# The sixth conditioning part moved into the output projection, the fifth spread over the last attention group, and earlier weight splits in the first stage

## The chip, the core and the metric

The kernel runs on one core of a Trainium2 chip. The metric is device time of one execution in microseconds (us), the median of several runs. Engines: TensorE does matrix products and transposes (PE in the profile, PEld its weight loads), VectorE is DVE, ScalarE is ACT, GpSimd is POOL, and SyncE (SP) issues most of the transfers from memory. Each engine works through its own instructions in the order in which they stand in its queue, and waits at an instruction whose inputs or buffers aren't ready.

## The reference, cut to what matters

One layer of a decoder for 512 prompt tokens and 8 x 4 sample tokens, 544 columns in all, with 1024 features. A conditioning vector c (one for the prompt, eight for the samples, nine in all) gives six modulation vectors:

```python
ada = jnp.einsum('bd,dn->bn', jax.nn.silu(c), lp['w_ada']) + lp['b_ada']
sh_m, sc_m, gt_m, sh_f, sc_f, gt_f = [a[:, None, :] for a in jnp.split(ada, 6, axis=-1)]
h = rms_norm(x, g[0]) * (1.0 + sc_m) + sh_m
y, st = mixer(h)                                  # projections, attention, convolution, merge, w_out
x = x + gt_m * rms_norm(y, g[1])
h = rms_norm(x, g[2]) * (1.0 + sc_f) + sh_f
a, b = jnp.split(jnp.einsum('btd,df->btf', h, lp['w_ffn_in']), 2, axis=-1)
y = jnp.einsum('btf,fd->btd', jax.nn.silu(a) * b, lp['w_ffn_out'])
x = x + gt_f * rms_norm(y, g[3])
```

`w_ada` is 1024 x 6144, 25 MB. Its six column blocks are the six conditioning parts, 0 to 5. Part 4 (sc_f, the fifth) is first needed in the second norm, after the output projection. Part 5 (gt_f, the sixth) is first needed when the last product of the feed-forward network is written out.

## The kernel before, in words

Data lie with features on the partitions and the 544 columns along the free dimension, in two halves of 272. Weights come as tiles of 128 x 1024 f32 (512 KB), through one ring, `RING`: a list of (planned time, kind, number), sorted by planned time. The tiles are loaded strictly in the ring's order. Each takes one of three `wraw` buffers (`NB = 3`); the odd conditioning tiles of parts 2 and 3 have a buffer of their own, `xraw`. The planned times are of a plan, not of the chip: TO, the start of the output projection in the plan, is 543.8, while its first products run near 579 us in the trace.

There are two sorts of ring tile:

- Weights of the big projections (glu, kv, g, pw2, q, gb, ga, out, fi, fo) are split in two before use: ACT writes a rounded high half `wh` (line 168), DVE the rest `wl` (line 171). Two `wh` and two `wl` buffers exist (the kept output tiles 5, 6 and 7 have three more of their own, which lie in memory that the attention gives back). A product of a half tile is 24 matmuls: high weights by high and low activations, then low weights by high activations. The `wraw` buffer is free for the next load when both halves are written.
- Raw tiles (`ada`, the conditioning tiles; `qs`; and a few more) are used by PE as they came. A conditioning tile is four 32-column matmuls (eight records in the trace) of the conditioning vectors by the tile. The buffer is free when PE is done with them. Eight tiles make a part: their sums collect in one buffer of PSUM that the part holds from its first to its last tile. Then ACT copies it (`adaz`, line 319), PE transposes the copy (`turn`), and DVE adds the bias into `adaT` (line 353).

What runs when is set by a heap of planned events: each step of each piece of work is a Python function with a planned time, and the instructions are emitted in the order of those times. In emission order earlier instructions have precedence; the final order on each engine can differ a little, since an instruction whose inputs are not expected yet is passed by others. The ring's bookkeeping runs along with the emission: `take` hands out the next tile, splits it if it isn't yet, and splits the next weight tile ahead if at most one raw tile lies between. `raw_done` gives a raw tile's buffer back. After a conditioning tile, `split_upto(rst["use"])` splits the next tile of the ring if that is a weight tile. `load_more` issues loads while there are buffers.

Around the change in time:

- First stage, to about 235 us: glu, kv and gate projections, a convolution of 31 steps for each of four channel groups on DVE (line 711), compression of cached pages, parts 2 and 3 and the `qs` tiles.
- Four attention groups (235 to 601 us). In each, four `unit`s of 128 rows: scores on PE into the two `big` buffers, mask and maximum on DVE (lines 1106, 1107), exponentials on ACT (line 1110), which free the `big` buffers, scaling (line 1118), transposes (line 1138, again into `big`), copies (lines 1139, 1140), products with the values into `pv`. Projections gb, ga, q and conditioning tiles are emitted between these steps. In the last group these are parts 4 and 5, with their sums in one of the two `mm` buffers.
- Output projection (from 579 us, overlapping the last unit): tiles `out0` 0 to 7 for the first column half, then the second half with kept tiles 5, 6, 7 (no loads) and `out1` 0 to 4. Their results go to `mm`. When the attention's memory is given back, SP loads x again (`load_x`, four transfers). The second norm and the feed-forward network follow.

Of the kernel before, what the change touches and what calls it, by code (L numbers as in the profile page):

```python
# [56 lines left out]
def at(g, x):  # L57

    t = TA + 14 + sum(GL[:g])
    return t + x * GL[g] / 10 if x <= 10 else t + GL[g] + (x - 10) * 6.4  # L60


TO = at(3, 10.345)
# [12 lines left out]
def fo_entry(ft, kg):  # L76
    return (ft // 4 * 3 + kg) * 4 + ft % 4


def _plan():  # L80

    p = [(1 + 0.1 * n, "glu", n) for n in range(NG)]
    p += [(2.345 + 0.089 * n, "ada", n) for n in range(8, 12)]
    p += [(45.047 + 6.5 * (n - NG), "glu", n) for n in range(NG, 8)]
    p += [(76.104 + 10.023 * n, "kv", n) for n in range(12)]
    p += [(60.955 + 4.999 * n, "ada", 16 + n) for n in range(16)]
    p += [(at(3, 1.557 + 0.388 * n), "ada", 32 + n) for n in range(16)]
    p += [(164.548, "g", 0)]
    p += [(203.02 + 3.438 * n, "pw2", n) for n in range(8)]
    p += [(114.735 + 9.994 * n, "qs", n) for n in range(8)]  # L90
    p += [(TA + 6.676 * n, "q", n) for n in range(2)]
    for g in range(4):
        if g < 3:
            p += [(at(g, 6.173 if g == 0 else 5.336), "q", 2 * g + 2), (at(g, 9.783) - 1.608, "q", 2 * g + 3)]
        p += [(at(g, 12.132 + 0.267 * n) if g < 3 else at(3, 0.308 + 0.745 * n), "ga", 2 * g + n) for n in range(2)]
    for n, (g, x) in enumerate(((0, 1.6), (0, 3.4), (0, 4.8), (0, 8.0), (1, 4.5), (1, 7.7), (2, 4.5), (2, 7.7))):
        p += [(at(g, x), "gb", n)]
    p += [(TO + 3.069 * n, "out0", n) for n in range(8)]
    p += [(TO + 31.9 + 2.718 * n, "out1", n) for n in range(5)]
    p += [(TO + 50.404 + 3 * NF * hf + 2.986 * n, "fi%d" % hf, n) for hf in range(2) for n in range(NF)]  # L100
    p += [(TS + 0.008 * n, "sf", n) for n in range(NF, 44)]
    p += [(TG + 64.062 * hf + 7.662 * ft + 3.08 * kg, "fo%d" % hf, fo_entry(ft, kg))
          for hf in range(2) for ft in range(8) for kg in range(3)]
    return [(t + 1e-4 * i, kind, n) for i, (t, kind, n) in enumerate(sorted(p))]


RING = _plan()
WHEN = {e[1:]: e[0] for e in RING}
KV_ORDER = [0, 1, 2, 4, 3, 5]
# [3 lines left out]
def body(ctx, tc, xT, cT, cst, sel, vecs, b1row, wall, w1, pool_rows, kwin, vwin, convst, ptab,  # L113
# [6 lines left out]
    def ev(t, f, *a):  # L120
        count[0] += 1
        heapq.heappush(heap, (t, count[0], f, a))
# [44 lines left out]
    def hi(dst, src, scale=1.0):  # L167
        act.activation(dst, src, AF.Copy, scale=scale)  # L168

    def lo(dst, src, h, eng=None):  # L170
        (eng or dve).tensor_sub(dst, src, h.bitcast(F32))  # L171
# [20 lines left out]
    def is_raw(j):  # L192
        _, kind, n = RING[j]
        return kind in ("ada", "qs", "sf") or kind == "glu" and n < NG

    raws, splits = {}, {}
    rst = {"load": 0, "split": 0, "use": 0}

    def entry(i):

        _, kind, n = RING[i]
        kind = kind.rstrip("01")
        if kind == "ada":
            return wall[n // 2][:, (n % 2) * 1024:(n % 2) * 1024 + 1024], 1024
        if kind == "fo":
            part, m = divmod(n, 4)
            k = FO_K[part % 3][1] * 128
            return wall[FIRST["wfo"] + part * 2 + m // 2][:, (m % 2) * k:(m % 2) * k + k], k
        k = 512 if kind == "pw2" else 1024
        kind = {"qs": "q", "sf": "fi"}.get(kind, kind)  # L210
        per = 1 if kind == "g" else 2048 // k
        return wall[FIRST["w" + kind] + n // per][:, (n % per) * k:(n % per) * k + k], k
# [4 lines left out]
    def load_more(end=len(RING)):  # L217

        while rst["load"] < end:
            j = rst["load"]  # L220
            _, kind, n = RING[j]
            own = kind == "ada" and 15 < n < 32 and n % 2
            pl, tag, bufs = (xr, "xraw", 1) if own else (wp, "wraw", NB)
            if j < 4 + NG and j % 3:
                pl, tag, bufs = late_pools["araw"], "araw", 5
            if kind == "sf" and (n - NF) % 4 == 3:
                pl, tag, bufs = late_pools["sraw"], "sraw", 1
            if out[tag] == bufs:
                break
            out[tag] += 1  # L230
            rst["load"] = j + 1
            src, k = entry(j)
            raw = pl.tile([128, 1024], F32, name=tag, tag=tag, bufs=bufs)
            if j == 6 + NG:
                load_w1()
            nc.sync.dma_start(raw[:, :k], src)
            raws[j] = raw, k, tag

    def raw_done(*tags):
        for tag in tags:  # L240
            out[tag] -= 1
        load_more()

    def split_upto(i):
        while rst["split"] <= min(i, len(RING) - 1):
            j = rst["split"]
            rst["split"] = j + 1
            if is_raw(j):
                continue
            raw, k, tag = raws.pop(j)  # L250
            out[tag] -= 1
            own = RING[j][1] == "out0" and RING[j][2] in KEPT
            h, l = ((kp if own else wp).tile([128, 1024], F32R, name=w, tag=w, bufs=3 if own else 2) for w in ("wh", "wl"))
            hi(h[:, :k], raw[:, :k])
            m = 640 if RING[j][1] in () else k
            lo(l[:, :m], raw[:, :m], h[:, :m])
            if m < k:
                lo(l[:, m:k], raw[:, m:k], h[:, m:k], pool)
            splits[j] = h.rearrange("p (k m) -> p k m", m=128), l.rearrange("p (k m) -> p k m", m=128)

    def take(kind, n):

        i = rst["use"]
        rst["use"] = i + 1
        assert RING[i][1:] == (kind, n), (RING[i], kind, n)
        if is_raw(i):
            return raws.pop(i)[::2]
        split_upto(i)
        j = i + 1
        while j < len(RING) and is_raw(j):  # L270
            j += 1
        if j - i <= NB - 1:
            split_upto(j)
        load_more()
        return splits.pop(i)

    def when(kind, n):
        return WHEN[kind, n]
# [33 lines left out]
    def ada_product(p, k, raw):  # L312

        for q in range(4):
            mm(p[32 * q:32 * q + 32, 0:256], cs[:, k], raw[:, q * 256:q * 256 + 256], k == 0, k == 7)

    def ada_quarters(p):
        z = hp.tile([128, 256], F32, name="adaz", tag="adaz", bufs=2)
        act.activation(z, p[:, 0:256], AF.Copy)
        return z  # L320
# [7 lines left out]
    def ada_bias(part):  # L328
        return vc[:, V_BADA + 8 * part:V_BADA + 8 * part + 8].rearrange("p (q a) -> p a q", a=2)
# [6 lines left out]
        dve.tensor_add(adaT[:, 0:2, 2 * qt:2 * qt + 2], t, bias.to_broadcast([128, 2, 2, 9]))  # L336
        return ins

    def ada_part(part, bank):

        def step(k):
            raw, tag = take("ada", 8 * part + k)
            if k == 0:
                ada_ps[part] = bank()
            ada_product(ada_ps[part], k, raw)
            raw_done(tag)
            split_upto(rst["use"])
            if k == 7:
                z = ada_quarters(ada_ps.pop(part))
                ev(when("ada", 8 * part + 7) + 4.968, turn, z)  # L350

        def turn(z):
            dve.tensor_add(adaT[:, part].rearrange("p (q a) b -> p a q b", a=2), ada_turned(z)[1],
                           ada_bias(part)[:, :, :, None].to_broadcast([128, 2, 4, 9]))

        for k in range(8):
            ev(when("ada", 8 * part + k), step, k)
# [3 lines left out]
    def modulation(dst, part, gi, plus1):  # L361
        gb = gains[:, gi, :, None].to_broadcast([128, 8, 9])
        if plus1:
            dve.scalar_tensor_tensor(dst, adaT[:, part], 1.0, gb, op0=OP.add, op1=OP.mult)
        else:
            dve.tensor_mul(dst, adaT[:, part], gb)
# [76 lines left out]
    def load_w1():  # L443
        for kd in range(2):
            t_ = xp.tile([128, 2048], F32, name="w1t", tag="w1t%d" % kd)
            nc.sync.dma_start(t_, w1[:, kd])
            w1t.append(t_.rearrange("p (l m) -> p l m", m=128))
# [502 lines left out]
    n = 0  # L950
# [13 lines left out]
    for part in (2, 3):  # L964
        ada_part(part, half_big)
# [339 lines left out]
                                dst = dst.rearrange("p (b t) -> p b t", t=4)  # L1305
                                act.activation(dst, v[64 * h2:64 * h2 + 64, :, pr, h2, 2 * jj + jp, :], AF.Copy)

    for part in (4, 5):
        ada_part(part, P_mm)
    for f in range(8):  # L1310
        ev(when("q", f), q_tile, f)
        gb_tile(f)
# [76 lines left out]
    A2 = yp.tile([128, 8, 9], F32, name="A2")  # L1389
    G3 = yp.tile([128, 8, 9], F32, name="G3")  # L1390
    modulation(A2, 4, 2, True)
    modulation(G3, 5, 3, False)
    uh, ul = {}, {}
    h2p = ctx.enter_context(tc.tile_pool(name="h2p", bufs=1))
    h2h = h2p.tile([128, 8, T], F32R, name="h2h", tag="h2h")
# [166 lines left out]
    raw, split, bank, keep = {}, {}, {}, {}  # L1562
# [273 lines left out]
```

## Time and profile before

| | |
|---|---|
| time, median of 3 runs | 1038.76 us (1038.04 to 1040.9) |
| the profiled execution | 1035.17 us |
| its span, first to last instruction | 1033.3 us |
| PE busy | 1006.7 us, 97% |
| DVE, ACT, POOL busy | 71%, 51%, 13% |
| mean granted PE clock | 0.995 |
| read from memory, written | 149.38 MB, 16.81 MB |

A busy PE is not PE at its peak: matmuls are pipelined, and their ends are modelled. In a timeline row the columns are start, length, engine, line, operation, output<-inputs, shape and count, and in brackets the idle time of the engine before it and what ended it. "x8" merges eight instructions. A row of the chain of waits has start, length, and what the chain ran through.

### The profile page before, as it was taken

How to read it: one execution, taken by the hardware profiler on the slowest of the kernel's cores; microseconds unless marked ns; L12 is line 12 of the kernel's file. 1: busy time of each engine (PE TensorE's matmuls, PEld its weight loads, DVE VectorE, ACT ScalarE, POOL GpSimd, SP SyncE). 2: the span in 40 equal slices, each digit the busy share in tenths (PEclk: the TensorE clock that was granted, in tenths of full speed). 3: DMA queues.
4: the chain of work that ended last, by engine and by line, in shares of the span. 5: the costliest groups of instructions: out<-in, count | busy, mean ns of one | idle time of the engine just before them, and what ended most of it. 6: DMA issues, size and time to landing. Idle time of an engine off the chain costs nothing.

```text
span 1033.3 us, 21219 instructions
## 1 busy us (share of the span) xinstructions
PE 1006.7 (97%) x8488; PEld 908.3 (88%) x8488; DVE 730.8 (71%) x1356; ACT 529.4 (51%) x1174; POOL 130.8 (13%) x142
## 2 busy tenths in 40 slices
PE   9998999999999999999998999999999999999996
PEld 7898899999877777777874799999999999999996
DVE  5689996343675775766757748899888988544554
ACT  5332125465546456454535556756666666444442
POOL 0040100001244244243231000000000000000000
PEclk9999999999999999999999999999999999999998
DMA  9955865424344343424436454654323233555652
GB/s 353 392 162 198 286 196 175 146 79 142 140 144 161 106 144 125 161 83 157 150 124 203 144 209 134 219 165 142 112 93 104 101 101 105 210 175 183 203 177 84
DMA packets 52195, 167.57 MB, mean 162 GB/s; under 512 B 6224, under 2 KB 8672, under 8 KB 51712
## 3 DMA queue, kind: packets, MB, share of 16 engines
q1 hardware_dynamic: 41328, 131.38, 38.0%
q10 hardware_dynamic: 7056, 20.81, 5.6%
q0 software_dynamic: 3712, 14.02, 4.1%
q8 instruction: 67, 1.10, 0.4%
q14 instruction: 32, 0.26, 0.1%
HBM read 149.38 MB, written 16.81 MB: 161 GB/s over the span
## 4 chain that ended last, share of the span: by engine, by line
PE 84%; DMA 6%; DVE 5%; ACT 2%; issue 1%; SPq 0%; DVEq 0%; ACTq 0%
PE mm L165 51%; PE pv L165 11%; PE big L165 10%; PE pt L165 5%; DMA wraw<-in_wall_dram 4%; PE big L1138 3%; DVE cy L711 2%; PE big L609 1%; DMA first<-in_wall_dram 1%; DMA xraw<-in_wall_dram 1%; DVE wl L171 1%; PE mm L609 1%; DMA x<-in_xT_dram 1%; ACT Xc L824 1%; PE pv L538 0%
## 5 line engine op out<-in xcount | busy, mean ns | idle before, releaser
L171 DVE TENSOR_TENSOR wl<-wraw,wh 128x1024 fp32r<-128x1024 f32 (+1 forms) x135 | 156.3, 1159 | 130.8 <-ACT wh L168 116.3
L168 ACT ACTIVATE wh<-wraw 128x1024 fp32r<-128x1024 f32 (+1 forms) x183 | 166.0, 908 | 155.8 <-PE mm L165 94.3
L165 PE MATMUL mm<-hh,wh 128*128 128x272 f32 (+1 forms) x608 | 172.7, 311 | 0.5 <-ACT at L671 0.5
L165 PE MATMUL mm<-hl,wh 128*128 128x272 f32 (+1 forms) x608 | 167.4, 302 | 0.0
L165 PEld LDWEIGHTS mm<-hh,wh 128*128 128x128 f32 x608 | 116.1, 191 | 12.9 <-issue 5.9
L165 PEld LDWEIGHTS mm<-hl,wh 128*128 128x128 f32 x608 | 115.6, 190 | 5.8 <-issue 2.8
L165 PE MATMUL mm<-hh,wl 128*128 128x272 f32 (+1 forms) x608 | 100.4, 302 | 2.7 <-DVE wl L171 2.7
L165 PEld LDWEIGHTS mm<-hh,wl 128*128 128x128 f32 x608 | 85.4, 189 | 8.6 <-issue 3.0
L1110 ACT ACTIVATE PB<-big,mx 128x128 f32<-128x128 f32 (+3 forms) x128 | 66.1, 526 | 51.0 <-DVE mx L1107 45.9
L165 PE MATMUL mm<-uh,wh 128*128 128x272 f32 x352 | 90.2, 289 | 1.0 <-ACT wh L168 1.0
L165 PE MATMUL mm<-ul,wh 128*128 128x272 f32 x352 | 90.1, 288 | 0.0
L711 DVE SCALAR_TENSOR_TENSOR cy<-hist,vc,cy 128x512 f32<-128x512 f32 x120 | 88.6, 791 | 0.4
L165 PE MATMUL mm<-h2h,wh 128*128 128x272 f32 x328 | 77.4, 288 | 0.0
L1118 POOL TENSOR_SCALAR PB<-PB,mx 128x128 f32<-128x128 f32 (+3 forms) x56 | 60.7, 1099 | 78.2 <-DVE mx L1115 34.1
L165 PEld LDWEIGHTS mm<-uh,wh 128*128 128x128 f32 x352 | 66.4, 189 | 1.2 <-ACT wh L168 1.2
L165 PE MATMUL mm<-h2l,wh 128*128 128x272 f32 x260 | 66.6, 287 | 0.0
L165 PEld LDWEIGHTS mm<-ul,wh 128*128 128x128 f32 x352 | 66.2, 188 | 0.0
L165 PEld LDWEIGHTS mm<-h2h,wh 128*128 128x128 f32 x328 | 58.5, 188 | 0.0
L165 PE MATMUL mm<-h2h,wl 128*128 128x272 f32 x312 | 53.1, 288 | 0.5 <-ACT pv L1605 0.5
L165 PE MATMUL mm<-uh,wl 128*128 128x272 f32 x352 | 52.2, 288 | 0.0
L1107 DVE TENSOR_REDUCE mx<-big 128x2 f32<-128x256 f32 (+3 forms) x64 | 51.0, 816 | 0.5
L165 PEld LDWEIGHTS mm<-h2l,wh 128*128 128x128 f32 x260 | 48.9, 188 | 0.0
(489 smaller groups left out, 2212.0 us busy)
## 6 DMA issues: line engine op xcount, KB each, us to landing
wraw<-in_wall_dram SPq DMA_DIRECT2D x170, 512.0 KB, 4.2
X<-in_rows_dram SPq DMA_DIRECT2D x32, 256.0 KB, 5.0
wraw<-in_wall_dram SPq DMA_DIRECT2D x16, 384.0 KB, 3.7
first<-in_wall_dram SPq DMA_DIRECT2D x8, 512.0 KB, 10.2
xraw<-in_wall_dram SPq DMA_DIRECT2D x8, 512.0 KB, 6.5
kw<-in_kwin_dram ACTq DMA_DIRECT2D x8, 512.0 KB, 3.5
out_wk_dram<-kw ACTq DMA_DIRECT2D x8, 512.0 KB, 5.2
vw<-in_vwin_dram ACTq DMA_DIRECT2D x8, 512.0 KB, 3.5
```

The costliest lines, as they stand in the source:

```text
L165: pe.matmul(out, lhsT, rhs, start=start, stop=stop, **more)
L168: act.activation(dst, src, AF.Copy, scale=scale)
L171: (eng or dve).tensor_sub(dst, src, h.bitcast(F32))
L609: ins = pe.matmul(gl[f][hf][:, :HT], w[:, k], r[:, k, sl], start=k == 0 and part == 0, stop=k == 7 and part == 2).ins
L711: dve.scalar_tensor_tensor(y, hist[:, ct, k:k + TP], w, y, op0=OP.mult, op1=OP.add)
L824: act.activation(o, src[:, r], AF.Copy)
L1107: dve.tensor_reduce(mx[:, 0, r, 2 * jj:2 * jj + 2], sc[:, :, :w], axis=AX.X, op=OP.max, negate=True)
L1110: act.activation(P[r][:, :, j * 128:j * 128 + 128], sc[:, jp, :w].rearrange("p (k n) -> p k n", n=128), AF.Exp, bias=mx[:, 0, r, j:j + 1], ...
L1118: (dve if r or g == 3 and i > 1 else pool).tensor_scalar(v, v, m[:, j:j + 1], None, op0=OP.mult)
L1138: pe.transpose(p[:, x, j * 128:j * 128 + 128], P[r][:, kt, j * 128:j * 128 + 128], ident)
```

## The change

Three things are changed. Part 4 keeps its eight tiles in the last attention group, at twice the spacing in the plan. Part 5's eight tiles are planned from TO + 1.5 on, every 5.2 us, between the tiles of the output projection; its sums collect in a `big` buffer instead of an `mm` buffer, and the gate G3 is computed when the part is done instead of right after the attention. And `raw_done`, after any raw tile planned in the first stage, looks for the next weight tile beyond the raw ones: if no split tile is waiting and that one's load has been issued, it is split at once.

```diff
@@ _plan
-    p += [(at(3, 1.557 + 0.388 * n), "ada", 32 + n) for n in range(16)]
+    p += [(at(3, 1.557 + 0.776 * n), "ada", 32 + n) for n in range(8)]
+    p += [(TO + 1.5 + 5.2 * n, "ada", 40 + n) for n in range(8)]
@@ raw_done
             out[tag] -= 1
         load_more()
+        j = rst["use"]
+        while j < len(RING) and is_raw(j):
+            j += 1
+        if not splits and j in raws and RING[j][0] < 200:
+            split_upto(j)
+            load_more()
@@ ada_part
-    def ada_part(part, bank):
+    def ada_part(part, bank, then=None):
...
         def turn(z):
             dve.tensor_add(adaT[:, part].rearrange("p (q a) b -> p a q b", a=2), ada_turned(z)[1],
                            ada_bias(part)[:, :, :, None].to_broadcast([128, 2, 4, 9]))
+            if then:
+                then()
@@ last attention group
-    for part in (4, 5):
-        ada_part(part, P_mm)
+    ada_part(4, P_mm)
+    ada_part(5, P_sc, lambda: modulation(G3, 5, 3, False))
@@ after the attention
     modulation(A2, 4, 2, True)
-    modulation(G3, 5, 3, False)
```

With the planned times the ring's order in the last attention group becomes: conditioning tile 32, ga tiles 4 and 5, conditioning tiles 33 to 39, then output tile 0, conditioning 40, output 1, 2, conditioning 41, output 3, conditioning 42, output 4, 5, conditioning 43, output 6, 7, conditioning 44, 45, and, beside the second half, output 0, conditioning 46, output 1, 2, conditioning 47, output 3, 4.

## The prediction

> **What bounds the kernel now.** I read the page's busy line first, then busy time in stretches of 10 us, then what TensorE (PE) waited for, then the timeline around each gap.
>
> ```profile
> PE 1006.7 (97%) x8488; PEld 908.3 (88%) x8488; DVE 730.8 (71%) x1356; ACT 529.4 (51%) x1174; POOL 130.8 (13%) x142
> 80.00:90.00 10.00, 7.32 (x64) 6.56 (x63) 10.00 (x14) 1.86 (x4) 2.56 (x1) 1.00 0.61 205
> 110.00:120.00 10.00, 8.16 (x71) 7.09 (x68) 10.00 (x15) 2.13 (x4) 0.41 (x1) 0.97 0.96 319
> 120.00:130.00 10.00, 10.00 (x78) 9.25 (x77) 10.00 (x17) 1.86 (x3) 0.00 (x0) 0.86 0.74 237
> ...
> 540.00:550.00 10.00, 9.78 (x124) 7.04 (x124) 6.00 (x11) 2.80 (x6) 2.33 (x4) 1.00 0.29 92
> 550.00:560.00 10.00, 9.03 (x71) 5.36 (x71) 7.13 (x16) 7.02 (x32) 0.54 (x1) 1.00 0.65 213
> 560.00:570.00 10.00, 6.83 (x71) 3.09 (x69) 8.89 (x19) 6.40 (x19) 0.93 (x2) 1.00 0.80 270
> 570.00:580.00 10.00, 9.43 (x63) 4.91 (x63) 7.45 (x13) 3.64 (x6) 0.00 (x0) 1.00 0.36 122
> ...
> 610.00:620.00 10.00, 9.52 (x79) 9.08 (x78) 4.46 (x8) 5.45 (x9) 0.00 (x0) 1.00 0.75 282
> 620.00:700.00 80.00, 80.00 (x655) 80.00 (x654) 73.69 (x141) 55.27 (x99) 1.84 (x2) 1.00 0.53 174
> ```
>
> PE bounds it, 97% busy. In a window row the first number after the length is PE's busy time, and the numbers at the end are granted clock, DMA share and GB/s. The change moves PE work and leaves its amount alone, so the only thing it can alter is PE's idle time and clock. That is 2.68 us in 80:90, 1.84 us in 110:120 followed by a clock of 0.86, and 0.22+0.97+3.17+0.57 = 4.93 us in 540:580, the end of the last attention group. Then 0.48 us in 610:620, and none from 620 on. All I can win or lose is there, or in new gaps.
>
> **Part 1: the sixth conditioning part leaves the attention tail.** Rows of PE, and the one ACT row that sets the pace:
>
> ```profile
> PE mm L165 <- DMA wraw<-in_wall_dram: 3.5, 4, 1.1
> 550.97 1.06 PE L1138 MATMUL big<-c,PB 128*128 128x128 f32 x8 [1.19 <-ACT PB L1110]
> 560.07 1.07 PE L165 MATMUL mm<-wraw,cs 128*32 128x256 f32 x16
> 561.57 0.64 PE L165 MATMUL mm<-wraw,cs 128*32 128x256 f32 x8
> 562.94 0.62 PE L165 MATMUL big<-KL,QS 64*128 64x512 f32 x4
> 564.66 0.64 PE L165 MATMUL mm<-wraw,cs 128*32 128x256 f32 x8 [1.10 <-DMA wraw<-in_wall_dram]
> 565.95 0.64 PE L165 MATMUL mm<-wraw,cs 128*32 128x256 f32 x8 [0.39 <-DMA wraw<-in_wall_dram]
> 566.94 0.69 ACT L1110 ACTIVATE PB<-big,mx 128x512 f32<-128x512 f32 x1 [3.60 <-DVE mx L1107]
> 567.57 0.64 PE L165 MATMUL mm<-wraw,cs 128*32 128x256 f32 x8 [0.98 <-DMA wraw<-in_wall_dram]
> 568.45 1.09 PE L1138 MATMUL big<-c,PB 128*128 128x128 f32 x8 [0.24 <-ACT PB L1110]
> 570.57 0.62 PE L165 MATMUL mm<-wraw,cs 128*32 128x256 f32 x2 [1.03 <-DMA wraw<-in_wall_dram]
> 582.87 0.72 DVE L171 TENSOR_TENSOR ml<-m,mh 128x544 fp32r<-128x544 f32 x1
> 592.73 6.03 PE mm L165 x48
> ```
>
> PE waits 3.5 us for conditioning tiles here, and at first sight the change removes all of it. But the waits sit inside a gap of another making. The transposes at 568.45 still had to wait 0.24 us for the exponentials, which began at 566.94 after ACT had idled 3.60 us for DVE's maxima. Between the scores (the KL row, done 563.5) and 568.2, PE has nothing of the attention to do, and the conditioning tiles were what filled it, late as they were. Only the last wait, 1.03 us at 570.57, has the next transposes queued behind it and lies on the chain.
>
> What leaves and what comes: a conditioning tile is 1.07/2 = 0.53 us of PE, so the eight that leave take 4.3 us of filler. The fifth part, at double spacing, now has its tiles 38 and 39 where 44 and 46 stood. Four places in or beside a gap lose their tile (one near 549, one of the two at 560.07, those at 561.57 and 565.95): 4 x 0.53 = +2.1 us of idle. The wait at 570.57 goes: -1.0. In return the first projection tile is loaded eight tiles sooner. A half tile is 24 matmuls in 6.03/2 = 3.0 us, and its first 12 need only the rows split long before; the other rows come with the split at 582.87. So 0 to 1.5 us of new filler, if its weights are split by about 565. Sum: -0.4 to +1.1 us.
>
> To this comes the clock:
>
> ```profile
> 115.98:119.39 3.41, 1.57 (x20) 0.53 (x19) 3.41 (x5) 0.40 (x1) 0.00 (x0) 1.00 1.04 402
> 119.39:122.80 3.41, 3.41 (x15) 3.41 (x16) 3.41 (x7) 0.38 (x1) 0.00 (x0) 0.50 1.01 296
> ...
> 566.53:569.95 3.42, 1.78 (x20) 1.01 (x16) 2.86 (x5) 3.01 (x9) 0.00 (x0) 1.00 0.89 280
> ```
>
> After 3.41 us in which PE was busy 1.57 us, the clock stood at 0.50 for 3.41 us, 1.7 us lost; after 1.78 us busy in 566.53:569.95 it did not fall. A barer gap can cross that line: 0 to +1.7 us. The Trainium skill ("TensorE: Matmul & The Clock Gate", section on the HAM clock gate) says that the clock halves after at least one idle window of about 3.4 us. This trace disagrees: a gap of 1.84 us in such a window was enough. By that rule neither loss nor recovery of clock would hang on gaps of this size, and the sum below would be about +0.5 instead of 0.
>
> I take +0.7 for the tail: the middle of -0.4 to +1.1, and a fifth of the clock. Ends: -3.5 (every wait goes, nothing replaces it) and +2.8.
>
> **Part 2: its eight tiles in the output projection.** They add 4.3 us of PE there (moved, not new) and eight 512 KB loads in the ring's three raw slots. They hold one of the two `big` buffers instead of one of two `mm`. The last unit's 16 transposes, back to back today, then have one buffer: the second eight wait for two copies like the 591.78 row below, some 1.3 us with their hand-overs; projection tiles 2 and 3 are there to cover it (1.3 if they don't). The turn and G3, two short DVE instructions, have until the last product. The loads are what matters:
>
> ```profile
> 591.78 0.60 ACT L1139 ACTIVATE pT<-big 128x512 f32<-128x512 f32 x1 [2.12 <-PE big L1138]
> 598.76 2.33 PE pv L165 x20
> 597.12 0.33 SPq L236 DMA_DIRECT2D wraw<-in_wall_dram  x1
> 602.08 0.80 SPq L1385 DMA_DIRECT2D x<-in_xT_dram  x2
> 603.57 7.44 DMA wraw<-in_wall_dram
> 602.62 2.00 ACT L168 ACTIVATE wh<-wraw 128x1024 fp32r<-128x1024 f32 x2
> wraw<-in_wall_dram SPq DMA_DIRECT2D x170, 512.0 KB, 4.2
> ```
>
> Today projection tile 7 is loaded at 597.12, before the attention ends (call the end E, 601.1 by the 598.76 row). Then SP waits for the attention's memory and issues four loads of x; the ring load among them takes 7.44 us, where 4.2 us is usual. With conditioning tiles in the slots, tiles 6 and 7 are not loaded by E. PE's order from E is conditioning 42, projection 4 and 5, conditioning 43, projection 6 at E+0.5+6.0+0.5 = E+7.0, 7 at E+10.0. Tile 6 takes the slot that 42 frees at E+0.6: landed E+4.8, high half split by E+5.9, in time, if SP issues it ahead of x. Tile 7 takes the slot of tile 5, whose split needs attention memory (the 602.62 row): issued E+2.5 like the 603.57 load, landed E+10, split E+11: PE waits about 1 us, 2.3 with tile 6's bytes ahead of it. If tile 6 is behind x, it lands at E+10 and PE waits 4 us, tile 7 then nothing. The Trainium skill ("DMA: Bandwidth & Descriptors", "Queues, rings and completion order") has each engine take a ring's descriptors in order; the 7.44 us agree. I take +1.0; ends 0 and +4.0.
>
> **Part 3: ring weights split sooner.** In the ring's bookkeeping the clause moves seven splits, of the eighth glu tile and kv tiles 1 to 6, forward by about 5 us of the plan each. In the opening it moves the fourth glu tile's split forward and puts one conditioning load ahead of the page gathers on SP.
>
> ```profile
> PE mm L165 <- DVE wl L171: 2.7, 1, 2.7
> 101.37 1.06 ACT L168 ACTIVATE wh<-wraw 128x1024 fp32r<-128x1024 f32 x1 [1.48 <-PE mm L165]
> 105.14 1.21 DVE L171 TENSOR_TENSOR wl<-wraw,wh 128x1024 fp32r<-128x1024 f32 x1
> L236 SPq DMA_DIRECT2D wraw<-in_wall_dram x3: 338/339/356, 106.4 to 119.9; - x3
> 110.18 8.51 DMA xraw<-in_wall_dram
> 118.73 0.64 PE L165 MATMUL big<-xraw,cs 128*32 128x256 f32 x8 [1.84 <-DMA xraw<-in_wall_dram]
> DMA to landing us min/median/max: 5.2/6.8/8.5
> ```
>
> The 2.7 us wait at 83 is for the seventh glu tile, which is split with the tile before it in both kernels: 0. The kv splits are on time for PE, but the low half at 105.14 runs 2.7 us after its high half was done (102.4), behind convolution rows on a full DVE; an earlier place frees its slot up to 2.7 us sooner, and the load issued at 106.4 moves out of the way of the one at 110.18. That one took 8.51 us, and PE waited 1.84 for it. The shortest such load took 5.2 us. Between 0 and -(1.84+1.7) = -3.5, the clock included; the two loads only partly overlap, so I take half, -1.7. On the loss side: a split put earlier on DVE delays a convolution step or a row of the opening by 1.2 us; I count it at nothing because the same DVE work is only reordered, and +1.2 if PE should be waiting for that row.
>
> **Sum.** -1.7 + 0.7 + 1.0 = 0.0. The profiled execution took 1035.17 us (span 1033.3 and 1.9 around it), 3.6 below the runs' median of 1038.76; in their terms the forecast is 1038.8.
>
> **Rivals.** Faster: the waits were real and nothing takes their place. Part 3 gives up to -3.5 and the tail -3.5: 1031.8 us; half of it, 1035.3, is already measurable. For it: PE waits 5.3 us on these two loads in so many words. Against: the 0.24 us wait on exponentials behind the tail's last filler.
>
> Slower: projection tile 6 is queued behind the x loads. +4.0 there, with the tail at +0.7 and no early gain: 1043.5; with the clock, 1045.2. It decides as soon as tile 6's load is issued after E+1.1, when x is. For it: SP already stood 4.6 us at x in its queue today. Against: the slot is free half a microsecond before the memory is.
>
> Not doing what it says: the clause leaves the engines' order as it was; then part 3 is 0, the sum +1.7, 1040.5, still inside the third of a per cent.
>
> **How the numbers follow.** About 0.3%, 3.1 us, is what a measurement can tell from no change. Forecast, 1035.7 to 1041.9: 0.40. Faster rival and its partial forms: 0.34. Slower: 0.26. The range reaches to where a tenth is left on each side: 1032 to 1044.
>
> **What would show it.** Right: no PE wait for wraw in 555:572, but still 2 to 4 us idle there, released by ACT's PB or a split; a PE or ACT wait for wraw some 7 to 12 us after the last attention product; the xraw wait near 119 shorter. Wrong: tail idle under 2 us (faster), a wait of 3 us or more behind the x loads, or a second stretch at clock 0.50 (slower).

## The result and the profile after

The change makes the kernel slower: 1045.11 us median against 1038.76, ratio 1.0064, 95% interval 1.0048 to 1.0080, that is +6.6 us (5.0 to 8.3). The profiled execution took 1045.33 us, its span is 1043.6 us with a mean clock of 0.991; before it was 1035.17, 1033.3 and 0.995. The forecast was 1038.8, no change.

The page's busy line and busy time in stretches of the kernel after; columns as before (length, PE, PEld, DVE, ACT, POOL, granted clock, DMA share, GB/s):

```profile
PE 1009.9 (97%) x8488; PEld 909.4 (87%) x8488; DVE 728.2 (70%) x1356; ACT 527.8 (51%) x1174; POOL 130.7 (13%) x142
...
80.00:90.00 10.00, 8.35 (x72) 7.52 (x70) 10.00 (x14) 1.33 (x3) 2.54 (x1) 1.00 0.31 100
110.00:120.00 10.00, 8.84 (x81) 7.47 (x79) 10.00 (x13) 2.11 (x4) 2.57 (x2) 1.00 0.88 244
120.00:130.00 10.00, 6.22 (x41) 5.58 (x42) 9.69 (x15) 1.84 (x3) 0.00 (x0) 0.83 0.81 307
...
610.00:620.00 10.00, 8.20 (x71) 6.86 (x70) 3.16 (x4) 4.32 (x9) 0.00 (x0) 1.00 0.94 352
620.00:700.00 80.00, 78.42 (x646) 76.29 (x646) 67.77 (x134) 52.41 (x96) 1.84 (x2) 1.00 0.58 196
```

PE's work is the same 8488 instructions; its idle time moved. 110:130 lost 1.16 + 3.78 = 4.94 us of PE where it had lost 1.84. 610:700 lost 1.80 + 1.58 = 3.4 us where it had lost 0.48. 80:90 lost 1.65 against 2.68, a gain. The rows behind these numbers, from PE's timeline after:

```profile
41.95 0.39 PE L618 MATMUL mm<-hl,w0h 128*128 128x272 f32 x1 [0.71 <-DVE hl L599]
43.32 0.39 PE L618 MATMUL mm<-hh,w0h 128*128 128x272 f32 x1 [0.41 <-ACT hh L169]
85.30 0.89 PE L166 MATMUL mm<-hh,wl 128*128 128x272 f32 x5 [1.65 <-DVE wl L172]
123.78 0.88 PE L166 MATMUL big<-xraw,cs 128*32 128x256 f32 x8 [4.94 <-DMA xraw<-in_wall_dram]
611.83 0.40 PE L166 MATMUL mm<-mh,wh 128*128 128x272 f32 x1 [1.10 <-ACT wh L169]
615.79 0.39 PE L166 MATMUL mm<-mh,wh 128*128 128x272 f32 x1 [0.69 <-ACT wh L169]
644.05 0.40 PE L166 MATMUL mm<-mh,wh 128*128 128x272 f32 x1 [0.70 <-ACT ysq L1364]
651.44 0.40 PE L166 MATMUL mm<-h2h,wh 128*128 128x272 f32 x1 [0.88 <-ACT wh L169]
```

The first two waits are new, in the opening. The wait at 123.78 is the old one for `xraw` and 3.1 us longer. The last four are new, in the output projection and the first tile of the network behind it. In the tail of the attention no wait for `wraw` is left; these took its place (columns of the waits: us in total, times, longest; PE, 540 to 600 us):

```profile
PE big L1147 <- ACT PB L1119: 2.8, 4, 1.2
PE mm L166 <- ACT wh L169: 1.2, 1, 1.2
```

Three transfers on the chain of waits after are the counterparts of the waits at 123, 615 and 644 us (start, length):

```profile
112.12 11.61 DMA xraw<-in_wall_dram
605.77 8.88 DMA wraw<-in_wall_dram
634.97 7.67 DMA wraw<-in_wall_dram
```

One difference between the two profiled executions isn't the change's. The profile after shows half clock from 14.81 to 21.64 with PE fully busy, and its second conditioning part ends 1.5 us later for it; the profile before has full clock there. The move alone, whose opening is untouched, shows the same stretch at half clock, and a repetition of the kernel before has another one at 82 and full clock near 119 (the repetition's PE, in stretches):

```profile
82.40:89.23 6.83, 6.00 (x27) 6.00 (x28) 6.83 (x9) 1.34 (x2) 2.54 (x1) 0.50 0.52 193
119.39:122.80 3.41, 1.98 (x21) 1.38 (x18) 3.41 (x6) 0.44 (x2) 0.00 (x0) 1.00 0.85 314
```

So single executions of one program differ by such stretches, 1.7 or 3.4 us each, and what follows goes by the ratios of many runs.

### The profile page after: what moved, and what is told of

Its sections match the earlier page's. It is cut to its first block, busy times and chain, and to the rows that moved or that the text cites. A ratio compares the mean times of both kernels' runs of the same rounds, so it can differ in the third digit from the quotient of the medians.

```text
span 1043.6 us, 21220 instructions
## 1 busy us (share of the span) xinstructions
PE 1009.9 (97%) x8488; PEld 909.4 (87%) x8488; DVE 728.2 (70%) x1356; ACT 527.8 (51%) x1174; POOL 130.7 (13%) x142
## 4 chain that ended last, share of the span: by engine, by line
PE 87%; DVE 6%; DMA 3%; ACT 3%; issue 1%; another core or an unknown queue 0%; SPq 0%; DVEq 0%; ACTq 0%
PE mm L166 52%; PE pv L166 11%; PE big L166 11%; PE pt L166 5%; PE big L1147 4%; DMA wraw<-in_wall_dram 2%; DVE cy L720 1%; DMA xraw<-in_wall_dram 1%; PE big L618 1%; ACT PB L1119 1%; DVE wl L172 1%; PE mm L618 1%; PE pt L547 1%; ACT wh L169 1%; DVE mx L1116 0%
## 5 line engine op out<-in xcount | busy, mean ns | idle before, releaser
L172 DVE TENSOR_TENSOR wl<-wraw,wh 128x1024 fp32r<-128x1024 f32 (+1 forms) x135 | 158.5, 1174 | 134.7 <-ACT wh L169 119.6
```

## The experiments

Every ratio is against the kernel before, from five rounds on the same chip.

| run | ratio | 95% interval |
|---|---|---|
| ctl, the kernel before again | 0.9992 | 0.9980 to 1.0004 |
| clause_only | 1.0043 | 1.0028 to 1.0058 |
| clause_late | 1.0001 | 0.9985 to 1.0016 |
| clause_nokv1 | 0.9996 | 0.9981 to 1.0011 |
| clause_hold | 1.0031 | 1.0016 to 1.0046 |
| clause_outlate | 0.9993 | 0.9977 to 1.0008 |
| outlate | 0.9980 | 0.9965 to 0.9994 |
| move_only | 1.0030 | 1.0018 to 1.0043 |
| move_noload | 1.0007 | 0.9993 to 1.0020 |
| move_mid | 1.0011 | 0.9998 to 1.0024 |
| move_xq | 1.0043 | 1.0025 to 1.0060 |
| after_fix | 1.0016 | 1.0000 to 1.0033 |
| pool_g6 | 1.0028 | 1.0013 to 1.0043 |
| pool_g6kv1 | 1.0064 | 1.0041 to 1.0088 |

**The control.**

> The kernel before once more, for how far two profiled executions of one program lie apart. Every theory: 1038.8 us within 0.3%, ratio 1.000. If the opening's half clock (14.8 to 21.6 us in the profile after, full there before) belongs to the execution and not to the change, this profile may show another phase of the clock windows and another place of the half-clock stretch; if it belongs to the change, PE's second conditioning part ends at 32.1 us here as in the profile before.

1035.17 us median, no difference. Its profiled span is 1037.1 us against 1033.3, so one profile of this kernel is good to some 4 us.

**The two halves of the change.** `clause_only` is the kernel before with the six lines in `raw_done`; `move_only` has all the other lines of the diff.

> Part 3 alone: ring weights split as soon as a conditioning tile is done, the sixth part left in the attention tail. Theory A (the loss comes from SP's order in the opening and from the later xraw landing as well as from the output projection): +1.5 us at the second products of the opening, -1 at the seventh glu tile, +3 with the longer xraw wait near 119, so +2 to +4 us, 1041 to 1043. Theory B (only the move costs; the opening's difference is the clock's phase, the xraw landing is chance): -1.7 to 0 us, 1037 to 1039.

> Parts 1 and 2 alone: the sixth part in the output projection, ring weights split as before. Theory A: the tail gains 1.0 and the output projection with the start of the feed-forward loses 4.4, so +3.4 us, 1042.2. Theory B (the move is all of it): +6.3, 1045. Theory C (what the prediction summed): +1.7, 1040.5.

Both lose, clear of noise: the clause 4.5 us (0.0043 of 1035.55), the move 3.1. Together that is 7.6, and the whole change's 5.0 to 8.3 holds it. So theory B of both falls, in which one of the two would be all of it, and the early split, on which I had put the only gain, is the larger loss.

**Which of the early splits costs.**

```diff
-        if not splits and j in raws and RING[j][0] < 200:
+        if not splits and j in raws and 60 < RING[j][0] < 200:
```

> The early split alone, but only for weight tiles planned after 60, so the fourth glu tile of the opening is split where it was. Theory A (the clause loses at two places, 1.0 us in the opening and 3 us at the xraw load near 119): the opening's products of `second` come at the times of before, the 1 us of the opening is gone, +3 us beside before, ratio 1.003. Rival (the opening is the whole loss, since all that follows it is shifted): ratio 1.000 or below.

```diff
+        if not splits and j in raws and 60 < RING[j][0] < 200 and RING[j][1:] != ("kv", 1):
```

> As clause_late, and the second kv tile too is split where it was. In the trace of the clause alone that tile's low half stands 1.6 us later on VectorE than before (106.74 against 105.14), the load that waits for it is issued 1.7 us later, and the conditioning tile in xraw lands 3 us later. If that displaced split is the cause, the load is back at 106.4, the xraw wait is at most 2 us again, and the time is within 1 us of before. If any early split of kv tiles crowds the xraw load, it stays at +3.

Without the opening the clause costs nothing: theory A's +3 us fell. The reason is plainer than either theory. On VectorE these programs have exactly the order of the kernel before, on ACT too but for two neighbouring rows near 177 us; on SP one load stands a few places earlier. The splits of the eighth glu tile and of the kv tiles are emitted sooner and are put back to the same place in the final order. Nor did `clause_nokv1` test what it was made for, since the second kv tile's split had not moved in `clause_late` either. The whole of the clause is one split, the fourth glu tile's in the opening, and what follows from it.

**What follows from it.** In `clause_only` the fourth glu tile's low half begins at 38.3 us instead of 39.7, and the fifth's, which follows it, at 41.3 instead of 46.9, between the rows of the activations; the waits of 0.7 and 0.4 us at 42 and 43 above are there too. Of these 1.1 us 1.0 comes back at the seventh glu tile, whose wait near 83 is 1.7 us instead of 2.7. Downstream the order has changed as well. Rows from SP, VectorE and PE of `clause_only`:

```profile
106.32 0.39 DVE L687 SCALAR_TENSOR_TENSOR hist<-sg,at 128x240 f32<-128x240 f32 x1
106.64 0.18 DVE L688 SCALAR_TENSOR_TENSOR hst<-sg,at 128x32 f32<-128x32 f32 x1
106.74 1.21 DVE L171 TENSOR_TENSOR wl<-wraw,wh 128x1024 fp32r<-128x1024 f32 x1
...
108.03 0.34 SPq L236 DMA_DIRECT2D wraw<-in_wall_dram  x1
110.06 1.39 SPq L236 DMA_DIRECT2D xraw<-in_wall_dram  x1
...
121.70 1.08 PE L165 MATMUL big<-xraw,cs 128*32 128x256 f32 x8 [4.93 <-DMA xraw<-in_wall_dram]
```

The low half that was to come sooner stands behind two rows of the convolution's input, at 106.74; before, it was at 105.14. The load that waits for it goes from 106.4 to 108.03. The `xraw` load is issued at the same time as before, 110.06 against 110.18, but lands after 11.6 us instead of 8.5. The same 4.9 us wait stands in the three profiles that have the opening's split and the state transfers (4.93, 4.94 and 4.94 in clause_only, clause_hold and after); the kernel before, its repetition, clause_late and clause_nokv1 have 1.2 to 2.2.

**Is it the load that the early split lets in?** The first conditioning tile of part 2 is loaded at 39.5 instead of 54. Here it is held back:

```diff
-        while rst["load"] < end:
+        while rst["load"] < end and not (rst["hold"] and rst["load"] > 9):
...
-        if not splits and j in raws and RING[j][0] < 200:
+        if not splits and j in raws and RING[j][0] < 60:
             split_upto(j)
-            load_more()
+            rst["hold"] = True     # cleared when the next weight tile is taken
```

> The early split of the fourth glu tile in the opening alone, but the load that its freed buffers allow (the first conditioning tile of part 2, issued at 39.5 in the clause alone against 54.1 before, ahead of the page gathers on SP) is held back until that glu tile is used. Theory A2 (the clause's 4.5 us come from that load: it keeps a ring buffer from 39 us on, though its tile is used at 78, so that the next ring loads come 5 us late, and everything on SP behind it): 0 to +1.5 us beside before, ratio 1.000 to 1.0015. Rival (the split itself pushes the activations' rows on ACT and VectorE, and with them the order of all that follows): it stays at +3.5 to +4.5, ratio 1.0035 or more.

1.0031, with the 4.94 us wait unchanged. Theory A2 falls: it had 1.0015 at most. The estimate is a quarter below that of `clause_only`, and the two intervals overlap, so what that load itself costs isn't resolved.

**Is it the crowd of transfers?** Two transfers write the convolution's states, 60 and 544 KB, at 107 and 110 us. A sum with zero times the convolution's result makes them wait for it:

```diff
-        nc.gpsimd.dma_start(o_conv, hist[:, :, TP:TP + 30])
-        nc.gpsimd.dma_start(o_convs, hst)
...
         dve.tensor_add(acc, acc, cy[:, 3])
+        for e in (hist[:, 0, TP:TP + 1], hst[:, 0, 0, 0:1]):
+            dve.scalar_tensor_tensor(e, acc[:, 0:1], 0.0, e, op0=OP.mult, op1=OP.add)
+        nc.gpsimd.dma_start(o_conv, hist[:, :, TP:TP + 30])
+        nc.gpsimd.dma_start(o_convs, hst)
```

> The clause alone with the same later issue of the two state transfers. In the clause alone PE waits 4.93 us for the xraw load near 119, against 1.2 to 2.2 us without it. Theory D (the clause's loss is mostly this wait, from crowded transfers): the wait falls to 1 to 2.5 us, and the time to between 0 and +2.5 us beside before, ratio 1.000 to 1.0025 against 1.0043. Rival E (the loss is in the opening, 39 to 53 us, and the xraw wait only shifts what is waited for): it stays at 1.004.

> The kernel before with one edit: the two transfers that write the convolution's states (60 and 544 KB, issued by POOL at 107 and 110 us, in the crowd ahead of the xraw load) are issued after the convolution's sum, near 205 us. Theory D (the xraw wait is the crowd of transfers between 106 and 120, of which the 544 KB one moves at 66 to 130 GB/s): the xraw load lands about 2 us sooner, the wait of 1.2 to 2.2 us near 119 goes, and with it the half clock behind it where there is one, -1.5 to -3 us, ratio 0.997 to 0.9985. Rival (the load's place in SP's order sets it): 1.000.

With the two transfers out of the way (they went at 171 to 175 us, sooner than the 205 expected), the clause is level with the kernel before: 0.9993 against 1.0043, intervals apart. Everything in the opening is as it was in `clause_only`, and its wait for the kv tile's buffer too, so rival E falls. But the same edit also speeds up the kernel before: `outlate` took 1034.09 us against 1035.67, ratio 0.9980 (0.9965 to 0.9994), as theory D expected. The fair pair is therefore 0.9993 against 0.9980. PE's idle time in the stretches in which the clause acts shows the same:

| PE idle, us | 24 to 60 | 60 to 100 | 114 to 124 | sum |
|---|---|---|---|---|
| before | 0.58 | 2.69 | 1.84 | 5.11 |
| clause_only | 1.72 | 1.66 | 4.93 | 8.31 |
| outlate | 0.58 | 2.67 | 0.03 | 3.28 |
| clause_outlate | 1.74 | 1.66 | 1.54 | 4.94 |

With the state transfers in their old place the clause costs 3.2 us of idle time and 4.5 us by the ratios; with them moved it costs 1.7 and 1.3, and the 1.3 isn't clear of noise. So theory D holds for a part of the loss, 1.5 us by idle time and about 3 by the ratios. The rest stays with the early split, at the same load: 1.54 us of wait against none. PE and SP rows of `clause_outlate`, and then two of its stretches of 2 us:

```profile
118.17 0.64 PE L165 MATMUL big<-xraw,cs 128*32 128x256 f32 x8 [1.54 <-DMA xraw<-in_wall_dram]
...
107.90 0.34 SPq L236 DMA_DIRECT2D wraw<-in_wall_dram  x1
109.92 0.37 SPq L236 DMA_DIRECT2D xraw<-in_wall_dram  x1
```

```profile
110.00:112.00 2.00, 2.00 (x17) 2.00 (x17) 2.00 (x4) 0.00 (x0) 0.00 (x0) 1.00 0.59 115
114.00:116.00 2.00, 2.00 (x18) 1.85 (x16) 2.00 (x4) 0.23 (x1) 0.00 (x0) 1.00 1.02 410
```

The same two stretches of `clause_only`:

```profile
110.00:112.00 2.00, 2.00 (x16) 2.00 (x17) 2.00 (x3) 0.00 (x0) 0.52 (x1) 1.00 0.88 66
114.00:116.00 2.00, 2.00 (x18) 1.99 (x16) 2.00 (x4) 1.35 (x2) 0.00 (x0) 1.00 1.04 404
```

The load is issued at the same time, the wait is 1.54 us instead of 4.93, and the load lands 3.5 us earlier. The size of the two transfers doesn't account for that. 604 KB at the 404 GB/s of the later stretch would be 1.5 us, and their own packets (`clause_only`, 100 to 122 us: packets, MB, share of the time of 16 transfer engines) come to 7.5% of 22 us, 1.65 us:

```profile
q0 software_dynamic: 176, 0.62, 7.5%
```

In 110:112 the transfer engines of `clause_only` were busier (0.88 against 0.59) and moved less (66 against 115 GB/s), but not with these transfers: all 32 packets of that stretch are of SP's queue, at 0.88 us of an engine each, against 0.25 us for the 75 packets of `clause_outlate`. The second transfer, issued at 109.91, moves its first packets only near 115. The Trainium skill ("DMA: Bandwidth & Descriptors", "Queues, rings and completion order") says that each transfer engine takes turns between the queues it has work for. Taking turns with these packets would cost a load some 1.65 us at most, an estimate from the row above, and the load landed 3.5 us sooner without them. That transfers of POOL's queue delay loads of SP's queue is shown; why SP's packets were slow in that stretch is open.

`outlate` is also the version that beats both kernels. PE's `xraw` product, the second row, starts there without a wait, and the next waits lie behind it (the waits of PE, 100 to 240 us):

```profile
116.61 0.64 PE L165 MATMUL big<-wraw,cs 128*32 128x256 f32 x8
117.28 0.64 PE L165 MATMUL big<-xraw,cs 128*32 128x256 f32 x8
...
PE mm L165 <- DVE wl L171: 1.8, 1, 1.8
PE pt L165 <- ACT qz L907: 1.1, 1, 1.1
```

**What in the move costs.** `move_noload` puts another operand under the sixth part's products and has no loads for them (it leaves out that part's result); `move_mid` plans the eight tiles behind the eighth output tile; `move_xq` issues x from POOL's queue:

```diff
+    p += [(TO + 22.2 + 1.9 * n, "ada", 40 + n) for n in range(8)]     # move_mid
...
-        nc.sync.dma_start(x1[:, k:k + 2], ...)
+        nc.gpsimd.dma_start(x1[:, k:k + 2], ...)                      # move_xq
```

> As the move alone, but the sixth part's eight tiles are not loaded: its products read the attention's hS in their place, as many and as large, at the same places, so the ring has eight loads fewer. The part's result is left out. If the loss behind the attention is the loads' (projection tiles pushed behind the x loads and split late), the waits on wh near 611 and 615 go and the time falls to 1037 to 1039. If it is the second `big` buffer or the place of the products, the waits stay and it is within 1 us of the move alone.

> The move alone, but the sixth part's eight tiles are planned from TO + 22.2 on, every 1.9, behind the eighth output tile, in place of from TO + 1.5 every 5.2. Theory A (the loss is projection tiles pushed back behind conditioning loads and the x loads at the end of the attention): no wait on wh between 590 and 625, +0 to +1 us beside before, 1035.5 to 1036.5. Rival (the ring is short of slots wherever the eight loads stand): the waits move to the second half, 630 to 655, and it stays at +3.

> The move alone with the four x loads issued from POOL's queue instead of SP's. If ring loads are late because they stand behind x in SP's queue, they are issued as their slots come free, the waits on wh near 611 and 615 go, and the time is +0.5 to +1.5 us beside before. If it is the slots or the shared bandwidth, the waits stay: +3.

Without the loads the move's loss is gone (+0.7 us, interval -0.7 to +2.1), and the products, the `big` buffer and the new tail are still there. With the loads behind the eighth output tile the waits on `wh` between 590 and 625 are gone, and the estimate is +1.1; its interval overlaps that of the move alone. With x on another queue the loss stays (1.0043): that loads stand behind x in SP's queue isn't the cause by itself, and this guess of mine fell. PE's waits there, 1.0 us at 609 and 1.7 at 617, are put down to `ysq`, but the chain of waits runs through ring loads of 7.36 and 5.31 us. So the loads at that place are the cause; whether by the ring's slots or by the shared transfer engines, these runs don't separate. PE's busy time in two stretches, the tail of the attention and the output projection, before:

```profile
540.00:600.00 60.00, 55.06 (x487) 38.22 (x489) 42.73 (x78) 31.48 (x83) 3.79 (x6) 1.00 0.47 158
600.00:660.00 60.00, 59.52 (x486) 58.52 (x483) 46.62 (x89) 39.14 (x74) 1.78 (x2) 1.00 0.54 186
```

the move alone:

```profile
540.00:600.00 60.00, 55.52 (x467) 40.29 (x467) 42.50 (x81) 32.34 (x84) 3.86 (x6) 0.97 0.34 112
600.00:660.00 60.00, 57.19 (x450) 53.61 (x449) 37.30 (x74) 32.27 (x64) 0.96 (x1) 0.94 0.64 217
```

without the loads:

```profile
540.00:600.00 60.00, 54.54 (x466) 40.19 (x465) 43.90 (x81) 33.85 (x85) 2.69 (x4) 0.97 0.32 101
600.00:660.00 60.00, 60.00 (x504) 57.15 (x503) 44.65 (x85) 36.76 (x72) 1.84 (x2) 1.00 0.53 183
```

In the tail PE idles 4.9, 4.5 and 5.5 us: the move gains nothing there, loads or not. In the output projection it idles 0.5, 2.8 and 0 us, and the move alone lost two stretches of 3.41 us to half clock besides (0.94 of 60 us).

**Both places undone in the changed kernel.** Clause as in `clause_late`, sixth part as in `move_mid`:

> The changed kernel with both disputed places undone and the rest kept: the early split only for tiles planned after 60, and the sixth part planned from TO + 22.2 on, every 1.9. If the opening's split and the loads ahead of output tiles 6 and 7 are the whole of the +6.6 us: 0 to +2 us beside before, ratio 1.000 to 1.002. If the two parts hold another loss together that neither has alone: above 1.003.

1.0016 (1.0000 to 1.0033), +1.7 us: some 5 of the 6.6 us come back. The two places carry most of the loss; a rest of 0 to 3.4 us isn't resolved.

**The wait at 83 by itself.** POOL writes the low half of the seventh glu tile, and in the second kernel that of the second kv tile too:

```diff
-            m = 640 if RING[j][1] in () else k
+            m = 0 if RING[j][1:] == ("glu", 6) else k
```

> The kernel before with one edit: the low half of the seventh glu tile, for which PE waits 2.7 us at 83, is written by POOL instead of VectorE. The prediction counted this wait as untouched by the change; here it is taken away by itself. If the wait is on the path: POOL's subtraction of 128x1024 takes about 2.6 us (from its 2.49 for 128x992) from 76.3 on, done by 79, the wait goes, -2.7 us and up to 1.7 us of half clock behind it, ratio 0.996 to 0.9975. Rival (PE meets another wait at once, or VectorE is slowed by POOL beside it): 0.999 to 1.000.

> As the last one, and the low half of the second kv tile also on POOL: it is then done near 105 instead of 106.35, without a convolution step before it, the load that waits for its buffer comes up to 1.4 us sooner, and the xraw load behind it too. If the xraw wait near 119 is set by that split, 1 to 1.5 us more than the last kernel, ratio lower by 0.001 to 0.003 (with the half clock behind the wait). If it is set by the bandwidth that all loads share there, no difference.

Both are slower, by 0.28% and 0.64%, where a gain was expected. POOL and VectorE rows of `pool_g6`:

```profile
76.62 6.17 POOL L171 TENSOR_TENSOR wl<-wraw,wh 128x1024 fp32r<-128x1024 f32 x1 [6.93 <-ACT wh L168]
...
80.51 2.83 DVE L712 SCALAR_TENSOR_TENSOR cy<-hist,vc,cy 128x512 f32<-128x512 f32 x1
```

The subtraction took 6.17 us, not 2.6, and a convolution step beside it 2.83 us, where its neighbours take 0.74. The wait at 83 shrank only to 1.9, others of 2.2 us at 111 and 1.4 us at 132 were new, and the one of 1.84 us near 119 is gone. These sum to 5.5 us against 4.5 before, so they aren't the whole loss of 2.9; the rest was not pursued.

## Why the prediction was wrong, by its own steps

- **What bounds the kernel: right.** All that was won or lost was PE's idle time and clock; PE's work stayed 8488 instructions.
- **Part 1, the tail, +0.7: right in kind.** The DMA waits in 555:572 went and others took their place, as said: released by ACT's `PB` and a split, 3.4 us in the kernel after and 2.1 in the move alone, within the 2 to 4 that were forecast. Idle time in 540:600 is within 0.6 us of before in the move alone and without loads. The half clock that a barer gap could bring came in the move alone (0.97 in 540:600), but the repetition of the kernel before has it too, at 570.5, so it takes no move to bring it.
- **Part 2, +1.0: mis-sized, the move costs 3.1 us in all.** The order of issue was as worked out: projection tile 6 ahead of x, tile 7 behind two loads of x, at 605.77. The size of the transfers was not. I let tile 6 land after 4.2 us, the median of all such loads. In the profile after it was issued near 604.0, and the split that its landing released began at 610.72, so it took some 6.7 us; tile 7 took 8.88. Both run beside each other and beside three of the loads of x: from 604 to 611 us the transfer engines were busy 0.84 of the time (0.94 before, whose one ring load there took 7.44 us), and the median of the whole run is no measure. I had read these 7.44 us as a place in the queue behind x; with x on another queue (`move_xq`) a ring load there takes 7.36. Two waits that followed in the second half, 0.7 us at 644 and 0.9 at 651, I had at nothing. (The rival "Slower: tile 6 behind x" meets the measured time, 1043.5 to 1045.2 against 1045.1, by luck: the tile was issued ahead of x, and the larger part of the loss came from part 3.)
- **Part 3, -1.7: the step that failed, measured +4.5 us.** Its first half fell because the forward move of the splits was read from the ring's bookkeeping. That is emission; the engines' final order put them back, and the gain is 0 (0.9985 to 1.0016). The rival "the clause leaves the engines' order as it was" describes this half. Its second half was one sentence: the opening's split and load, counted at nothing. The bound that I gave it, +1.2 if PE waits for a delayed row, was what the opening itself cost, 0.7 + 0.4 us, and 1.0 of it came back at 83. The larger cost lay 65 us later, at the very load that I had priced as a gain: half of a recovered wait of 1.84 became 3.1 us more of it. I had read that load as late because of what stood ahead of it in SP's order. That may be a part: with the state transfers moved, the wait is 1.54 us where the clause issues the load ahead at 107.90, and none in `outlate`, where that load goes at 106.74. The other part, 3.4 of the 4.93 us with the clause and the whole 1.84 without, went with two transfers of POOL's queue that I hadn't looked at.
- **The clock.** That a gap of less than a window of 3.41 us can halve the clock held: it stood behind the wait of 1.84 us in the kernel before, and it came within one of 2.86 that ended at 83.2 in the repetition (the 4.9 us waits of clause_only and after are longer than a window). But busy time draws no clear line, as I had drawn one between 1.57 and 1.78 us. In windows counted from the repetition's own fall at 82.42, PE was busy 2.66 us in 614.91:618.32, and the clock fell next; after the 1.78 us of 566.53:569.95 in the kernel before it hadn't. The repetition's wait near 120 falls into two such windows, with 3.03 and 2.37 us busy, and the clock stayed. The Trainium skill ("TensorE: Matmul & The Clock Gate", "What's actually happening") says that the window runs freely, and so the same kernel meets it at another phase; the half clock at 119 in one execution and at 82 in the other agrees.

Of the three signs of being right, two came: no wait for `wraw` in 555:572, and ACT's waits for `wraw` that ended at 610.72 and 614.68, 7 and 11 us after the last attention product at 603.4. The third, a shorter `xraw` wait, came out longer.

The upper end, 1044, came from one rival alone. Added up without any early gain, the tail's +0.7, the output projection's +4.0 and the opening's +1.2 give 1044.7, still below the measured 1045.1: the 3.1 us at the `xraw` load stood in no bound.

## What to carry to other kernels

An emission order is not the order on the engines: look at where an instruction ends up before pricing a move forward, and price a moved load by the transfers that are under way where it will run, not by the median of the run. When PE waits for a load, list every transfer in flight in that window on every queue; taking an unhurried write out of it (here 604 KB of states) was worth 0.2% of this kernel. When an edit is tried on a changed kernel, try it on the kernel before as well, or its own gain is taken for the cure. A conditioning tile as filler moves a wait; its 512 KB come along, and they cost where other loads are under way.

## What the runs showed of the hardware that was not expected

- Transfers of POOL's queue slowed a load of SP's queue by more than their bytes and their own packets (1.5 and 1.65 us): the `xraw` load took 11.6 us with the two state transfers beside it and 8.2 without, issued within 0.2 us of the same time.
- POOL and VectorE held each other up: a subtraction of 128x1024 on POOL took 6.17 us beside the convolution, a convolution step 2.83 instead of 0.74 us. A second such subtraction, in `pool_g6kv1` at 102.54, took 2.81. The Trainium skill ("SBUF — State Buffer", "Who interferes with whom") describes a pair of ports that the two share under an exclusive lock, and has a VectorE instruction with two inputs in SBUF contend with a GpSimd instruction that reads SBUF; the first pair of rows agrees.
- Two profiled executions of one program differed by 3.8 us of span and had their stretches of half clock, but for the last 12 us, at different places: 3.41 us at 119 in one; 6.83 us at 82 and 3.41 each at 570 and 618 in the other. The kernel after was at half clock from 14.8 to 21.6 us with PE fully busy.
